# The low parts of the up product's first unit made on GpSimd in place of VectorE, in 54 of 56 expert groups

## The chip, the cores and the metric

The kernel runs on one core of one Trainium2 chip. The metric is the device time of one execution in microseconds (us); below, all times are us unless they say ns. A core has TensorE (PE; its weight loads are shown apart as PEld), VectorE (DVE), ScalarE (ACT), GpSimd (POOL) and SyncE (SP, which here issues the weight transfers). Each engine takes its own instructions in order, and they wait for one another through semaphores. SBUF is the working memory of all of them; PSUM holds what TensorE writes.

## The reference, cut to what matters

Two residual blocks run over 256 tokens of width 1024: first two mLSTM and attention layers, then two layers with a gated mixer each, the first with a dense feed-forward part and the second with a mixture of experts. The change lies in the experts:

```
def moe_swiglu(x, w_router, e_gate, e_up, e_down):
    ...
    top_val, top_idx = lax.top_k(logits, TOP_K)          # 2 of 8 experts for each token
    ...
    for e in range(N_EXPERTS):
        out = out + gates[:, e:e + 1] * swiglu(t, e_gate[e], e_up[e], e_down[e])

def swiglu(x, w_gate, w_up, w_down):
    return (jax.nn.silu(x @ w_gate) * (x @ w_up)) @ w_down
```

The width is 1024, an expert's hidden width 3584, and everything is float32.

## The kernel before

TensorE multiplies parts of float32 numbers. A weight tile `raw` (128 by 2048, 1 MB, called a unit here) is split in two: ScalarE writes its high part, `hi = Copy(raw)` in a shorter format (`high`, L1381), and VectorE writes the remainder, `lo = raw - hi` (`low`, L1385). A product of an expert with many tokens then takes three matmuls for each 128 rows (`mm3`, L242 to L244: hi by x high, lo by x high, hi by x low). For an expert with at most 64 tokens both parts of x lie side by side in one operand, and two matmuls do (L1355 and L1356); two more with a folding matrix (L1406) add up the halves. Which of the two forms runs is a branch on a number computed on the chip.

The expert stage works in 56 **groups**: 8 experts by 7 slices of 512 hidden columns. The list `turns` pairs the experts and alternates between the two of a pair, so that a group of a crowded expert stands beside one of a small expert. A group needs six units: two of the gate matrix (k = 0, u = 0 and 1), two of the up matrix (k = 1) and two of the down matrix (k = 2). They are made in this order; `some(n)` makes the last of group n + 1, the down units of group n and the first three of group n + 2:

```
    high(n + 1, 1, 1); low(n + 1, 1, 1); up(n + 1, 0)
    high(n, 2, 0); turn_hidden(n); high(n, 2, 1); low(n, 2, 0)
    up(n + 1, 1); low(n, 2, 1)
    high(n + 2, 0, 0); low(n + 2, 0, 0); high(n + 2, 0, 1); down(0)
    low(n + 2, 0, 1); high(n + 2, 1, 0); down(1)
    low(n + 2, 1, 0); activate(n + 1)
```

(This is the order without the other steps; the whole function is below.) The stage is recorded under `manual_schedule` for VectorE, ScalarE and TensorE, so these three engines keep the written order. Beside the six `lo`, VectorE does two things in a group, and both read one operand in PSUM: `activate` multiplies the gate by the up product (L1412, `tmp<-tmp,mm`), and `turn_hidden` makes the low part of the transposed hidden tile (L299, `yl<-mm,yh`). A `lo` reads two operands in SBUF. Where a new pair of experts begins there is more: its tokens are picked and gathered (L1285, L1291, L1305 to L1307), and the results of the pair before are added in (`combine`, L1430 and L1431).

The buffers are four `hi`, four `lo` and seven `raw` (four and three in two pools, picked in turn by `raw_tile`). A raw buffer is free when its `lo` is made, and then SyncE issues the next transfer into it (L204). A `hi` or `lo` buffer is free when TensorE has used it. GpSimd has nothing to compute in the expert stage.

Of the kernel before, what the change touches and what calls it, by code (L numbers as in the profile page):

```python
# [10 lines left out]
F32 = mybir.dt.float32  # L11
# [4 lines left out]
OP = mybir.AluOpType  # L16
# [1199 lines left out]
def moe(E, G, p, l, i, out):  # L1216
    nc, tc, I = E.nc, E.tc, E.I
# [150 lines left out]
    raws, w = {}, {}  # L1368
# [13 lines left out]

    def low(n, k, u):
        hi, lo = (x.rearrange("p k n -> p (k n)") for x in w[n, k, u])
        return nc.vector.tensor_tensor(lo, raws.pop((n, k, u)), hi.bitcast(F32), op=OP.subtract)  # L1385

    FIRST = 2
    state = {}
# [53 lines left out]
    for e in range(NEXP):  # L1442
        todo = lambda n, f, *a, of=ahead: of.setdefault(n, []).append((f, a))
        if e:

            n = at[e - 2, nf - 1] - 1 if e > 1 else 0
# [6 lines left out]
        if e % 2 and e + 1 < NEXP:  # L1453
            n = at[e, nf - 1] + 1
# [3 lines left out]
    def some(n):  # L1458
# [19 lines left out]
        if nxt:  # L1478
            high(n + 1, 1, 1)
            low(n + 1, 1, 1)  # L1480
            up(n + 1, 0)
# [3 lines left out]
        turn_hidden(n)  # L1485
        high(n, 2, 1)
        low(n, 2, 0)
        beside_hidden(n)
        if nxt:
            up(n + 1, 1)  # L1490
        low(n, 2, 1)
        if nxt2:
            high(n + 2, 0, 0)
# [202 lines left out]
```

## Time and profile before

| | |
|---|---|
| Time, median of 3 runs | 2000.57 us (2000.23 to 2000.99) |
| Profiled execution: time | 2002.43 us |
| Profiled execution: span, first to last instruction | 2000.1 us |
| TensorE, VectorE, ScalarE, GpSimd busy | 1927.3, 1550.2, 1374.1, 75.7 us |
| The 56 groups, from the first L1412 to the last | 1103.3 to 1971.4 us |
| Expert weights read | 336 units of 1 MB |

A busy time is the union of an engine's instructions. Over the whole span it mixes stages with different limits, so the expert stage is read in stretches of its own. There GpSimd is idle, and TensorE, VectorE, ScalarE and the DMA engines are all busy for most of the time; which of them is waited for changes between stretches. The name in brackets behind a timeline row says what an engine's idle time before that row ended with.

### The profile page before, as it was taken

The page shows a single profiled execution, that of the slowest core. Times are in us where ns is not written, and L with a number is a line of the kernel's source. Part 1 is how long each engine was busy: PE and PEld are TensorE (multiplying, and loading weights), DVE is VectorE, ACT ScalarE, POOL GpSimd, SP SyncE. Part 2 cuts the span into 40 slices and gives each one's busy share as a digit, 9 for nine tenths or more (in the row PEclk, how much of TensorE's full clock was granted, in tenths as well). Part 3 has the DMA queues.
Part 4 walks back from the last instruction along what each step waited for, and adds up shares of the span by engine and source line. Part 5 has one row for each costly group of instructions (what it writes and reads, how often), then busy time and mean ns, then how long its engine had stood idle before and what let it go on. Part 6 is the DMA issues. An engine that isn't in the chain of part 4 may idle for free. (4 is left out here: it accounts for less than half of the span.)

```text
span 2000.1 us, 28105 instructions
## 1 busy us (share of the span) xinstructions
PE 1927.3 (96%) x10164; PEld 1602.2 (80%) x10164; DVE 1550.2 (78%) x1992; ACT 1374.1 (69%) x1932; POOL 75.7 (4%) x109
## 2 busy tenths in 40 slices
PE   8999999999999999999998999999999999999886
PEld 7778998977999887999887787777878787776664
DVE  7857555976555676555867899889999899999996
ACT  7656455756544564444555789888898888989994
POOL 0100000010000210000010000000000000000000
PEclk9999999999999999999998999999999999999998
DMA  7515544534555563555443899999999999999993
GB/s 271 203 43 189 190 169 150 198 132 137 185 187 176 192 220 113 203 211 189 178 171 128 344 398 419 415 357 389 418 418 381 361 418 419 404 358 407 419 420 158
DMA packets 77208, 536.95 MB, mean 268 GB/s; under 512 B 9102, under 2 KB 9376, under 8 KB 13296
## 3 DMA queue, kind: packets, MB, share of 16 engines
q1 hardware_dynamic: 75312, 528.52, 68.7%
q0 software_dynamic: 1296, 6.02, 0.9%
q8 instruction: 111, 1.82, 0.4%
q14 instruction: 57, 0.47, 0.1%
q10 hardware_dynamic: 432, 0.12, 0.0%
HBM read 533.58 MB, written 1.05 MB: 267 GB/s over the span
## 5 line engine op out<-in xcount | busy, mean ns | idle before, releaser
L1385 DVE TENSOR_TENSOR lo<-raw,hi 128x2048 fp32r<-128x2048 f32 x333 | 745.2, 2283 | 33.4 <-ACT hi L1381 33.4
L1381 ACT ACTIVATE hi<-raw 128x2048 fp32r<-128x2048 f32 x333 | 633.6, 1919 | 30.2 <-PE mm L244 12.2
L1041 DVE TENSOR_TENSOR lo<-raw,hi 128x512 fp32r<-128x512 f32 (+2 forms) x696 | 428.2, 666 | 159.4 <-ACT hi L1040 158.9
L1040 ACT ACTIVATE hi<-raw 128x512 fp32r<-128x512 f32 (+2 forms) x696 | 372.5, 602 | 200.0 <-issue 88.8
L243 PE MATMUL acc<-lo,yh 128*128 128x512 f32 x656 | 257.6, 393 | 4.1 <-DVE lo L1385 3.9
L242 PE MATMUL acc<-hi,yh 128*128 128x512 f32 x656 | 258.1, 393 | 0.0
L244 PE MATMUL acc<-hi,yl 128*128 128x512 f32 x656 | 256.5, 391 | 0.0
L190 PE MATMUL mm<-xh,hi 128*128 128x256 f32 x736 | 208.5, 283 | 0.0
L191 PE MATMUL mm<-xl,hi 128*128 128x256 f32 x736 | 208.3, 283 | 0.0
L192 PE MATMUL mm<-xh,lo 128*128 128x256 f32 x736 | 208.3, 283 | 0.0
L242 PE MATMUL mm<-hi,xh 128*128 128x512 f32 x432 | 172.3, 399 | 2.1 <-PEq L1510 1.7
L1355 PE MATMUL mm<-hi,yl 128*128 128x512 f32 x416 | 166.2, 400 | 5.1 <-PEq L1510 4.3
L243 PE MATMUL mm<-lo,xh 128*128 128x512 f32 x432 | 169.3, 392 | 1.6 <-issue 1.6
L244 PE MATMUL mm<-hi,xl 128*128 128x512 f32 x432 | 169.2, 392 | 0.0
L1356 PE MATMUL mm<-lo,yl 128*128 128x512 f32 x416 | 163.1, 392 | 0.0
L243 PEld LDWEIGHTS acc<-lo,yh 128*128 128x128 f32 x656 | 123.4, 188 | 32.9 <-DVE lo L1385 9.0
L244 PEld LDWEIGHTS acc<-hi,yl 128*128 128x128 f32 x656 | 123.2, 188 | 25.2
L242 PEld LDWEIGHTS acc<-hi,yh 128*128 128x128 f32 x656 | 123.5, 188 | 24.7
L191 PEld LDWEIGHTS mm<-xl,hi 128*128 128x128 f32 x736 | 141.2, 192 | 0.6
L190 PEld LDWEIGHTS mm<-xh,hi 128*128 128x128 f32 x736 | 141.2, 192 | 0.6
L192 PEld LDWEIGHTS mm<-xh,lo 128*128 128x128 f32 x736 | 141.2, 192 | 0.0
L242 PE MATMUL acc<-hi,xh 128*128 128x512 f32 x288 | 116.7, 405 | 1.0 <-ACT xh L298 0.6
(339 smaller groups left out, 3055.8 us busy)
## 6 DMA issues: line engine op xcount, KB each, us to landing
raw<-in_exp_w_up_dram SPq DMA_DIRECT2D x112, 1024.0 KB, 8.6
raw<-in_exp_w_gate_dram SPq DMA_DIRECT2D x112, 1024.0 KB, 8.2
raw<-in_exp_w_down_dram SPq DMA_DIRECT2D x112, 1024.0 KB, 8.0
raw<-in_w_in_dram SPq DMA_DIRECT2D x48, 1024.0 KB, 5.0
raw<-in_w_up_dram SPq DMA_DIRECT2D x32, 1024.0 KB, 4.9
raw<-in_w_down_dram SPq DMA_DIRECT2D x32, 1024.0 KB, 4.8
raw<-in_w_out_dram SPq DMA_DIRECT2D x16, 1024.0 KB, 4.9
raw<-in_ffn_w_gate_dram SPq DMA_DIRECT2D x10, 1024.0 KB, 5.6
```

The costliest lines, as they stand in the source:

```text
L190: nc.tensor.matmul(out, lhsT=wh, rhs=ah, start=start, stop=False)
L191: nc.tensor.matmul(out, lhsT=wh, rhs=al, start=False, stop=False)
L192: nc.tensor.matmul(out, lhsT=wl, rhs=ah, start=False, stop=stop)
L242: nc.tensor.matmul(out, lhsT=ah, rhs=wh, start=start, stop=False)
L243: nc.tensor.matmul(out, lhsT=ah, rhs=wl, start=False, stop=False)
L244: nc.tensor.matmul(out, lhsT=al, rhs=wh, start=False, stop=stop)
L1040: a = E.nc.scalar.activation(hi, v, AF.Copy)
L1041: return a, E.nc.vector.tensor_tensor(lo, v, hi.bitcast(F32), op=OP.subtract)
L1355: nc.tensor.matmul(out, lhsT=a[2][:, k, :], rhs=wh, start=f, stop=False)
L1356: nc.tensor.matmul(out, lhsT=a[2][:, k, :], rhs=wl, start=False, stop=l)
L1381: nc.scalar.activation(w[n, k, u][0].rearrange("p k n -> p (k n)"), raws[n, k, u], AF.Copy)
L1385: return nc.vector.tensor_tensor(lo, raws.pop((n, k, u)), hi.bitcast(F32), op=OP.subtract)
```

## The change

`low` chooses its engine. For the first unit of the up matrix, (k, u) = (1, 0), in groups 2 to 55 the subtraction is issued on GpSimd; in groups 0 and 1, and for all other units, it stays on VectorE. Operands and result are the same.

```
     def low(n, k, u):
         hi, lo = (x.rearrange("p k n -> p (k n)") for x in w[n, k, u])
-        return nc.vector.tensor_tensor(lo, raws.pop((n, k, u)), hi.bitcast(F32), op=OP.subtract)
+
+        on = nc.gpsimd if (k, u) == (1, 0) and n >= FIRST else nc.vector
+        return on.tensor_tensor(lo, raws.pop((n, k, u)), hi.bitcast(F32), op=OP.subtract)
```

The file is two lines longer from there on: L1385 becomes L1387, L1412 becomes L1414, and so on. In the following rows, in a steady part of the stage, `lo1601` is the low part that moves, `lo1599` the second gate unit of the same group and `lo1604` the last unit of the group before; `tmp1602` is the product that `activate` makes. VectorE before:

```order
L1385 TENSOR_TENSOR lo1599_14726<-raw1598_14723,hi1599_14725 128x2048
L1361 UNCONDITIONAL_BRANCH
L1385 TENSOR_TENSOR lo1601_14753<-raw1600_14750,hi1601_14752 128x2048
L1412 TENSOR_TENSOR tmp1602_14780<-tmp1602_14780,mm1594_14671 128x512
L1385 TENSOR_TENSOR lo1604_14786<-raw1603_14783,hi1604_14785 128x2048
```

VectorE with the change, at the same place:

```order
L1387 TENSOR_TENSOR lo1599_14726<-raw1598_14723,hi1599_14725 128x2048
L1361 UNCONDITIONAL_BRANCH
L1414 TENSOR_TENSOR tmp1602_14780<-tmp1602_14780,mm1594_14671 128x512
L1361 UNCONDITIONAL_BRANCH
L1387 TENSOR_TENSOR lo1604_14786<-raw1603_14783,hi1604_14785 128x2048
```

VectorE now goes from the second gate unit to the product, and then to the next group's unit; nothing else on it changes its place among the computing instructions. GpSimd with the change, with the semaphores that each row waits for; before, only the branches stood here:

```order
L1361 UNCONDITIONAL_BRANCH x2
L1387 TENSOR_TENSOR lo1601_14753<-raw1600_14750,hi1601_14752 128x2048 [waits DMAHW4_49,Activation_49,Pool_49]
L1361 UNCONDITIONAL_BRANCH x4
L1512 UNCONDITIONAL_BRANCH
L1361 UNCONDITIONAL_BRANCH x2
L1387 TENSOR_TENSOR lo1619_14935<-raw1618_14932,hi1619_14934 128x2048 [waits DMAHW2_49,Activation_49,Pool_49]
```

The moved subtraction has GpSimd to itself, and it starts when ScalarE has made its `hi`. TensorE's order is unchanged; its first matmul with `lo1601` and SyncE's transfer into the freed raw buffer now wait for GpSimd where they waited for VectorE.

## Rows read from the trace of the kernel before

**Rows 1.** Busy engines by stretch of the expert stage, PE clock, DMA share
```profile
core 0: us, PE busy (x) PEld busy (x) DVE busy (x) ACT busy (x) POOL busy (x), PEclk, DMA share, GB/s
1144.00:1265.10 121.10, 118.98 (x536) 96.19 (x535) 115.87 (x65) 108.87 (x92) 0.00 (x0) 1.00 1.00 409
...
1487.70:1590.50 102.80, 101.36 (x476) 81.28 (x475) 91.65 (x60) 89.91 (x85) 0.00 (x0) 1.00 0.96 373
1590.50:1710.40 119.90, 117.67 (x529) 94.97 (x528) 115.71 (x66) 107.49 (x91) 0.00 (x0) 1.00 1.01 418
1710.40:1797.10 86.70, 85.66 (x404) 68.57 (x403) 76.96 (x51) 76.05 (x72) 0.00 (x0) 1.00 0.97 376
1797.10:1883.90 86.80, 79.78 (x341) 58.73 (x339) 86.54 (x50) 80.48 (x70) 0.00 (x0) 1.00 1.00 411
1883.90:1959.70 75.80, 66.44 (x270) 47.33 (x270) 72.67 (x42) 68.53 (x57) 0.58 (x1) 1.00 1.01 420
```

**Rows 2.** Timeline of VectorE over two groups: start, length, instruction, idle before
```profile
1634.85 0.68 DVE L1412 TENSOR_TENSOR tmp<-tmp,mm 128x512 f32<-128x512 f32 x1
...
1638.76 0.69 DVE L299 TENSOR_TENSOR yl<-mm,yh 128x512 fp32r<-128x512 f32 x1 [1.03 <-ACT yh L298]
1639.37 11.13 DVE L1385 TENSOR_TENSOR lo<-raw,hi 128x2048 fp32r<-128x2048 f32 x5
1650.42 0.68 DVE L1412 TENSOR_TENSOR tmp<-tmp,mm 128x512 f32<-128x512 f32 x1
...
1653.82 11.09 DVE L1385 TENSOR_TENSOR lo<-raw,hi 128x2048 fp32r<-128x2048 f32 x5
1664.83 0.68 DVE L1412 TENSOR_TENSOR tmp<-tmp,mm 128x512 f32<-128x512 f32 x1
```

**Rows 3.** Who waited for the lo of L1385, 1144 to 1960: us, times
```profile
  PE acc L243: 3.9, 9
  PE acc L1356: 3.1, 9
  PE mm L1356: 0.8, 1
```

**Rows 4.** What VectorE waited for, 1487.7 to 1590.5: us, times, longest
```profile
DVE lo L1385 <- ACT hi L1381: 7.6, 4, 3.1
DVE yl L299 <- ACT yh L298: 2.2, 4, 1.0
DVE X L1431 <- PE mm L1430: 1.3, 2, 1.0
```

**Rows 5.** Timeline of GpSimd in earlier stages, multiplications with two operands in SBUF
```profile
70.81 0.73 POOL L486 TENSOR_TENSOR tmp<-tmp,rope 128x256 f32<-128x256 f32 x1 [2.96 <-ACT tmp L480]
80.37 2.27 POOL L486 TENSOR_TENSOR tmp<-tmp,rope 128x256 f32<-128x256 f32 x1 [7.94 <-ACT tmp L480]
685.43 1.30 POOL L864 TENSOR_TENSOR ws<-ws,tri 128x512 f32<-128x512 f32 x1 [0.27 <-DMA ws<-in_wsT_dram]
716.27 1.46 POOL L910 TENSOR_TENSOR gg<-gg,srow 128x512 f32<-128x512 f32 x1
720.21 1.30 POOL L864 TENSOR_TENSOR ws<-ws,tri 128x512 f32<-128x512 f32 x1 [2.49 <-DMA ws<-in_wsT_dram]
```

**Rows 6.** Timeline of VectorE at those times
```profile
80.77 0.68 DVE L485 TENSOR_TENSOR tmp<-tmp,rope 128x512 f32<-128x512 f32 x1
81.37 0.68 DVE L1041 TENSOR_TENSOR lo<-raw,hi 128x512 fp32r<-128x512 f32 x1
685.30 1.29 DVE L299 TENSOR_TENSOR xl<-mm,xh 128x512 fp32r<-128x512 f32 x2 [0.34 <-ACT xh L298]
715.88 3.64 DVE L1041 TENSOR_TENSOR lo<-raw,hi 128x512 fp32r<-128x512 f32 x4
```

**Rows 7.** Timeline of ScalarE: the hi of (0,1) and (1,0), then the activation
```profile
1644.07 3.71 ACT L1381 ACTIVATE hi<-raw 128x2048 fp32r<-128x2048 f32 x2
1647.67 0.59 ACT L1411 ACTIVATE tmp<-mm 128x512 f32<-128x512 f32 x1
```

## The prediction, made before the changed kernel was run

> **What bounds the kernel now.** I read the busy times by stretch first, because the whole-span shares mix stages. The change touches only the 56 expert groups, so I cut these at the starts of their L1412 rows. In the steady stretches [rows 1] (1590.5 to 1710.4, eight groups; the one from 1367.9 to 1487.7 is like it, and 1144.0 to 1265.1 nearly) TensorE is busy 98% of the time, VectorE 97%, and the DMA engines move 418 GB/s at a share of 1.01. All three look like the limit. The stretches in which a new pair of experts starts (1487.7 to 1590.5, six groups; 1265.1 to 1367.9 is the same; 1710.4 to 1797.1, five groups) have TensorE at 99% and VectorE at 89%. In the last eleven groups (1797.1 to 1959.7) TensorE falls to 92 and 88% while VectorE has 99.7 and 96%.
>
> VectorE's timeline [rows 2] shows how close it is. The five `lo` in a row take 11.09 us: one is 2.28 us long, and start to start it is (11.09 - 2.28) / 4 = 2.20 us. L1412 and L299 take 0.6 us each, start to start (1638.76 to 1639.37). Six `lo` and these two make 6 x 2.2 + 1.2 = 14.4 us, and the group from 1650.42 to 1664.83 is 14.41 us long: VectorE had no pause at all. The group before took 15.57 us, with one pause of 1.03 us. So VectorE is a bound in these groups, and anything that adds to its line adds to the time; TensorE and DMA follow within a few per cent.
>
> **The change, part by part.** Removed: 54 `lo` on VectorE, 2.2 us each in its line, 119 us in all. Added: 54 subtractions of 128x2048 on GpSimd, which is idle there. No row of before has that operation at that size. The nearest are multiplications with two SBUF operands [rows 5]: 128x256 in 0.73 us and 128x512 in 1.30 us, so (1.30 - 0.73) / 256 = 2.23 ns a column and 0.16 us at the start. For 2048 columns that is 4.7 us; I take 4.6 us of it as the work itself (below). On its own this would be harmless: the result is used a group later.
>
> The question is what VectorE does meanwhile, and the earlier stages show it. At 715.88 VectorE ran four `lo` of 128x512 [rows 6]. Four that are undisturbed would take 3 x 0.6 + 0.68 = 2.48 us; they took 3.64, which is 1.16 us more. GpSimd's multiplication of 128x512 [rows 5] began at 716.27, while the first of them ran. It lasted 1.46 us, 0.16 us more than alone, and ended at 717.73. So GpSimd first waited for the `lo` in progress, and then VectorE stood for GpSimd's whole working time: 1.16 us for 512 columns, 2.27 ns a column. Neither ran beside the other. For 2048 columns that makes 4.6 us. At 685.30 it was otherwise: two VectorE subtractions whose first operand is in PSUM (L299) took 1.29 us for two, so 0.6 us each as elsewhere, right beside GpSimd's L864 [rows 5, 6]. So I take it that a `lo`, with both operands in SBUF, and the new GpSimd subtraction exclude one another, and that L299 and L1412 do not mind.
>
> Where in the group does the 4.6 us fall? GpSimd can start when its `hi` is made. In the group of [rows 2] ScalarE made the `hi` of (0,1) and (1,0) from 1644.07 on and was done at 1647.78 [rows 7]. VectorE's five `lo` began at 1639.37, so the fourth, of (0,1), ran from 1645.97 to 1648.2 and the fifth, the moved one, from 1648.2. GpSimd is thus ready while the fourth runs and gets its turn at 1648.2, just where VectorE's own would have started. VectorE can then run L1412 (0.6 us, PSUM) and stands before the next `lo`. Its line per group is five `lo` (11.0), L1412 and L299 (1.2) and 4.6 for GpSimd, less the 0.6 of L1412 beneath it: **16.2 us in place of 14.4, +1.8 us**. The pauses of about 1 us for `yh` in every other steady group go away, since VectorE then comes later than TensorE. The waits that move to GpSimd (TensorE's first matmul with this `lo`, SyncE's next transfer, a later `hi` of ScalarE) come most of a group after GpSimd is done, and are costed at nothing; a group that is over 1 us longer also leaves the transfers more room.
>
> The sum by stretches: the three steady ones have 24 groups, 24 x 16.2 = 388.8 us against 121.1 + 119.8 + 119.9 = 360.8: **+28**. The last eleven groups last 162.6 us. 11 x 16.2 = 178.2 is +16; but both experts of this pair are small, TensorE is done with its buffers sooner, and GpSimd may be ready before the fourth `lo` begins. Then nothing is hidden and a group is 16.8 us, +22. I take **+19**. In the 17 groups of the three other stretches VectorE waits already, 11.1 us in six groups [rows 4]; GpSimd can work within such a wait. Of the six, one has no wait (+1.8) and one only 0.5 us (+1.3): at least 3 us a stretch, at most 6 x 1.8 = 10.8. I take 5, 5 and 4, together **+14**. The first two groups, which fill the pipeline, get nothing. Together 28 + 19 + 14 = +61 us. The profiled execution took 2002.4 us (span 2000.1), so 2063 us; the median of the runs is 1.9 us lower, and the forecast for it is **2062 us**.
>
> **Two rules of the Trainium skill against these rows.** Its page "GPSIMD Engine Reference" (section 3, Performance versus the Vector engine) gives 4497 ns for a float32 addition of this size on GpSimd, which would be 0.1 us less a group than my 4.6, some 4 us less in the sum. Its page "SBUF — State Buffer" (SBUF: two separate sides) says that VectorE with two SBUF inputs and GpSimd share a pair of ports as a lock, which whoever starts first holds for its whole instruction. The trace agrees on the standing still (1.16 us for 512 columns), but not on the turn: at 80.37 GpSimd's 128x256 took 2.27 us in place of 0.73, while two VectorE instructions that started after it, at 80.77 and 81.37, ran at their usual 0.68 [rows 5, 6]. By first come, the last pair costs 22 and the total is 64; if VectorE may go ahead as at 80.37, GpSimd gets in at L1412 in every group, the last pair costs 16, and the total is 58.
>
> **Rivals.** *They do not exclude one another in this form* (the other side). VectorE's line would fall to 12.2 us a group. For it: the GpSimd rows are multiplications with float32 results, not subtractions to the shorter format. Against it: the 1.16 us above. The time would then go to the next limits. Six units are 6.29 MB; at the 418 to 420 GB/s of [rows 1] that is 15.0 us, and the steady groups take (15.57 + 14.41) / 2 = 14.99. So nothing is gained there: 1998 to 2001 us, no measurable change. It decides from the point where GpSimd's turn costs VectorE under 2.2 us.
>
> *Nothing is hidden*: L1412 stands too, or GpSimd's turn falls between two `lo` everywhere, and the waits in the gather stretches absorb nothing. Then a group is 16.8: 28 + 24 x 0.6 = 42, 17 x 1.8 = 31, and 22, so +95: 2096 us. *More is hidden*, L299 as well as L1412, 15.6 us a group: 24 x 15.6 = 374.4 (+14), 171.6 (+9), and some 4 in the gather stretches: +27, 2028 us.
>
> *Faster*: without exclusion and with DMA able to do more than these rows show, TensorE's own waits for `lo` could go, 7.8 us in all [rows 3]: 1993 us. Both conditions are needed, and 1.01 of DMA share speaks against the second.
>
> **How the numbers follow.** Exclusion with a group of 15.6 to 16.8 us: 0.86, most likely near 16.2, so 2062, with the bounds of the hidden part 2028 and 2096. No exclusion: 0.10 without a gain, 0.04 with one. The range leaves out the rivals without exclusion and the outer part of "nothing hidden": 2024 to 2092. A measurement of this kernel can tell about 0.2% (4 us) from no change. Faster 0.04, same 0.09, slower 0.87.
>
> **What would show it.** Right: GpSimd rows of about 4.6 to 5 us, or longer where they wait for their turn; one `lo` a group that takes 6 us or more in place of 2.28, the first behind L1414; steady groups of about 16.2 us without waits for `yh`; DMA at 6.29 MB / 16.2 us = 388 GB/s; TensorE waiting for `lo` more than before. Wrong: `lo` at 2.28 us beside a busy GpSimd; the long one behind L299 or in the middle of the five; groups in the gather stretches that grow as much as the steady ones. TensorE's clock shows 1.00, its 2.4 GHz level, in the last groups with TensorE at 88% [rows 1], about as idle as a group of 16.2 us would leave it (118 / 130 = 91%), so I expect no fall to 1.2 GHz; longer single waits would break that and make it slower still.

## The result, and the profile after

The changed kernel takes **2066.73 us** (median of 5 runs, 2063.84 to 2069.66), against 2000.57 us before (5 runs, 2000.23 to 2002.02): a ratio of 1.0333, with a 95% interval of 1.0322 to 1.0344. The forecast was 2062 us with a range of 2024 to 2092. The profiled execution of after is the fastest of its five (2063.84 us, span 2062.0), and its span is 61.9 us longer than the one of before.

L1387 is now the line of every `lo`, L1413 and L1414 are the activation's two lines (L1411 and L1412 before). Cut 0.04 us ahead of the starts of the L1414 rows, which end the same groups as the cuts of [rows 1], the stretches are these (columns as in [rows 1]):

```profile
core 0: us, PE busy (x) PEld busy (x) DVE busy (x) ACT busy (x) POOL busy (x), PEclk, DMA share, GB/s
1145.75:1272.68 126.93, 120.28 (x531) 95.24 (x530) 119.17 (x56) 108.52 (x92) 44.27 (x9) 1.00 0.97 378
...
1509.40:1617.91 108.51, 103.01 (x475) 80.70 (x474) 94.27 (x53) 89.85 (x85) 32.13 (x7) 1.00 0.92 350
1617.91:1746.11 128.20, 120.67 (x531) 95.12 (x530) 120.53 (x57) 108.56 (x92) 45.63 (x9) 1.00 0.99 392
1746.11:1840.63 94.52, 88.70 (x407) 69.03 (x406) 81.86 (x46) 78.47 (x73) 31.78 (x6) 1.00 0.93 353
1840.63:2018.03 177.40, 150.77 (x606) 113.11 (x606) 172.73 (x78) 145.92 (x127) 57.84 (x10) 0.94 0.98 381
```

The rows of eight groups went from 121.1 and 119.9 us to 126.9 and 128.2, those in which a pair of experts starts from 102.8 and 86.7 to 108.5 and 94.5, and the last eleven groups from 162.6 to 177.4. VectorE now makes one `lo` a group fewer, yet its busy time in eight groups rose (115.7 to 120.5 us). GpSimd, idle there before, is busy 5.7 us a group. TensorE fell from 98 to 94%, DMA from 418 to 392 GB/s. So neither of these two became the bound; VectorE's line got longer. Its timeline shows where:

```profile
1641.15 8.88 DVE L1387 TENSOR_TENSOR lo<-raw,hi 128x2048 fp32r<-128x2048 f32 x4
1649.96 0.68 DVE L1414 TENSOR_TENSOR tmp<-tmp,mm 128x512 f32<-128x512 f32 x1
1651.40 5.25 DVE L1387 TENSOR_TENSOR lo<-raw,hi 128x2048 fp32r<-128x2048 f32 x1 [0.77 <-ACT hi L1381]
1656.57 0.68 DVE L299 TENSOR_TENSOR yl<-mm,yh 128x512 fp32r<-128x512 f32 x1
1657.17 8.88 DVE L1387 TENSOR_TENSOR lo<-raw,hi 128x2048 fp32r<-128x2048 f32 x4
1665.98 0.67 DVE L1414 TENSOR_TENSOR tmp<-tmp,mm 128x512 f32<-128x512 f32 x1
```

GpSimd's timeline over the same group:

```profile
1649.21 5.29 POOL L1387 TENSOR_TENSOR lo<-raw,hi 128x2048 fp32r<-128x2048 f32 x1 [10.73 <-ACT hi L1381]
1664.45 6.09 POOL L1387 TENSOR_TENSOR lo<-raw,hi 128x2048 fp32r<-128x2048 f32 x1 [9.96 <-ACT hi L1381]
```

Read the two together. GpSimd asks at 1649.21 (its row of 5.29 us, against 4.56 for the shortest of them, holds a wait for its turn), while the last of VectorE's four `lo` runs. That `lo` ends at 1650.03 (1641.15 + 8.88), GpSimd's row at 1654.50: 4.47 us. In them VectorE does L1414 and then stands. Its next `lo` begins at 1651.40, ends at 1656.65, and has its usual 2.2 us only from about 1654.4 on. The four behind it are undisturbed (8.88 us for four). The group takes 16.02 us in place of 14.4 to 15.6.

The result has a reader sooner than forecast. TensorE's timeline of that group, its first matmul with the moved unit:

```profile
1654.55 0.50 PE L1356 MATMUL mm<-lo,yl 128*128 128x512 f32 x1 [1.18 <-POOL lo L1387]
```

TensorE had come to it 1.18 us before GpSimd was done. Its waits for the moved unit from 1150 to 2020 (us in total, times, longest):

```profile
PE mm L1356 <- POOL lo L1387: 37.2, 28, 1.9
```

What VectorE waits for in the six groups that start a pair (1509.4 to 1617.9; before: [rows 4]):

```profile
DVE tmp L1414 <- ACT tmp L1413: 5.9, 2, 3.0
DVE lo L1387 <- ACT hi L1381: 5.4, 7, 1.7
DVE X L1433 <- PE mm L1432: 1.6, 2, 1.0
DVE yl L299 <- ACT yh L298: 1.2, 1, 1.2
```

That is 14.1 us in all, where it was 11.1.

| stretch | before | after | difference | forecast |
|---|---|---|---|---|
| first two groups | 40.73 | 42.55 | +1.8 | 0 |
| three steady stretches, 24 groups | 360.84 | 383.32 | +22.5 | +28 |
| three gather stretches, 17 groups | 292.25 | 311.56 | +19.3 | +14 |
| last eleven groups | 162.58 | 177.40 | +14.8 | +19 |
| the last interval, group 54 to 55 | 11.68 | 15.53 | +3.9 | 0 |

The cut between the last two of the long stretches hides something: the first of the last eleven groups takes 12.60 us in place of 14.41. It is the sixth after a pair starts, and in the two other gather stretches the sixth took 13.99 in place of 15.9. Counted with its stretch, the gather groups cost 17.5 and the last ten groups 16.6.

### The profile page after: what moved, and what is told of

It is laid out like the page before. It is cut to its first block, busy times and chain, and to the rows that moved or that the text cites. A ratio compares the mean times of both kernels' runs of the same rounds, so it can differ in the third digit from the quotient of the medians.

```text
span 2062.0 us, 28109 instructions
## 1 busy us (share of the span) xinstructions
PE 1947.9 (94%) x10164; PEld 1609.1 (78%) x10164; DVE 1591.5 (77%) x1938; ACT 1375.4 (67%) x1932; POOL 374.9 (18%) x163
## 5 line engine op out<-in xcount | busy, mean ns | idle before, releaser
L1387 DVE TENSOR_TENSOR lo<-raw,hi 128x2048 fp32r<-128x2048 f32 x279 | 782.4, 2844 | 47.3 <-ACT hi L1381 47.3
L1387 POOL TENSOR_TENSOR lo<-raw,hi 128x2048 fp32r<-128x2048 f32 x54 | 300.0, 5556 | 610.4 <-ACT hi L1381 610.3
L1356 PE MATMUL mm<-lo,yl 128*128 128x512 f32 x416 | 171.9, 413 | 37.5 <-POOL lo L1387 27.8
L243 PEld LDWEIGHTS acc<-lo,yh 128*128 128x128 f32 x656 | 123.7, 189 | 37.8 <-DVE lo L1387 13.9
```

Source lines behind the costliest of these rows:

```text
L243: nc.tensor.matmul(out, lhsT=ah, rhs=wl, start=False, stop=False)
L1356: nc.tensor.matmul(out, lhsT=a[2][:, k, :], rhs=wl, start=False, stop=l)
L1387: return on.tensor_tensor(lo, raws.pop((n, k, u)), hi.bitcast(F32), op=OP.subtract)
```

## The experiments

The theory under test: GpSimd's two-operand subtraction and VectorE's `lo` exclude one another, so a moved column saves VectorE 1.04 ns (a `lo` of 128x512 takes 0.6 us of its line, one of 128x2048 2.2, so (2.2 - 0.6) / 1536) and costs it about 2.2 ns. The main rival: they don't, and the time comes from the result being late for TensorE, or from writes.

**GpSimd writes as long, but reads almost nothing** (e1_write_only). One column of the moved `lo` is subtracted, the others are filled; `behind` keeps each instruction after the one before. (In the edits below, `...` stands for lines left out.)

```diff
...
+        i = nc.gpsimd.tensor_tensor(lo[:, 0:1], raw[:, 0:1], hi[:, 0:1].bitcast(F32), op=OP.subtract)
+        for end in (2048, 2048, 768):
+            with behind(E, [i]):
+                i = nc.gpsimd.memset(lo[:, 1:end].bitcast(F32), 0.0)
```

> The moved subtraction is replaced on GpSimd by one column of it and three constant fills of the same tile (2047, 2047 and 767 columns), so the tile is ready about as late as with the change, but GpSimd reads almost nothing from SBUF; the product then works with fills in place of the low parts. Theory (VectorE stands while GpSimd reads two SBUF operands): VectorE's line falls to 12.2 us a group and its lo stay at 2.28 us; the next limit is DMA, 1996 to 2004 us. Rival (the tile comes late and TensorE waits for it): as with the change, 2062 to 2068 us. If a GpSimd write alone also stops VectorE: 2062 too, but with lo of over 5 us.

Measured: 2013.79 us, ratio 1.0067 (1.0051 to 1.0084). GpSimd's row and VectorE's rows beside it:

```profile
1444.89 4.50 POOL L1392 MEMSET lo<- 128x2047 f32 x3
```
```profile
1445.38 0.69 DVE L1419 TENSOR_TENSOR tmp<-tmp,mm 128x512 f32<-128x512 f32 x1 [0.47 <-ACT tmp L1418]
1447.18 2.29 DVE L1388 TENSOR_TENSOR lo<-raw,hi 128x2048 fp32r<-128x2048 f32 x1 [1.12 <-ACT hi L1381]
```

The `lo` at 1447.18 lies beside GpSimd's last two fills and takes its usual 2.29 us; of all 279 none took over 2.295. So a GpSimd that writes as long and is about as late costs 13 us, not 66. The theory had counted on 1996 to 2004 and missed the lateness: TensorE waits 32.8 us for GpSimd's tile in 31 places, and the three steady stretches are 3.9 us longer than before, the three gather stretches 5.9, the last interval 3.5.

**One fill** (e4_short_write): as above with a single fill, so GpSimd is done 2.7 us sooner.

```diff
-        for end in (2048, 2048, 768):
-            with behind(E, [i]):
-                i = nc.gpsimd.memset(lo[:, 1:end].bitcast(F32), 0.0)
+        with behind(E, [i]):
+            nc.gpsimd.memset(lo[:, 1:2048].bitcast(F32), 0.0)
```

> One fill of 2047 columns in place of the moved subtraction: VectorE is relieved of one lo a group, and the tile is ready about 2 us after its hi, sooner than before the change. It bounds what relieving VectorE of this lo could bring. If DMA at 419 GB/s is the next limit: 1995 to 2001 us. If VectorE alone was the limit: 24 groups down from 15.0 to 14.7 (TensorE's 29.4 a pair) and the last eleven from 14.8 to 12.8 or so: 1970 us.

Measured: 1995.51 us, 0.9978 (0.9969 to 0.9988), the steady stretches 4.0 us shorter than before. That is about all that freeing VectorE of one `lo` a group brings here: its line falls to 12.2 us a group, but the steady groups still take 14.9 on average. TensorE is 99% busy in them and DMA moves 419 to 420 GB/s, so there either can be the bound; in the last groups, of 14.9 us too, TensorE is at 88% and DMA at 419 GB/s. The run with three fills took 18 us more than this one: that is what 2.7 us of lateness cost without the exclusion.

**GpSimd copies in place of subtracting** (e2_one_input): the three fills of the first run become copies from `raw`, one operand to read.

```diff
-                i = nc.gpsimd.memset(lo[:, 1:end].bitcast(F32), 0.0)
+                i = nc.gpsimd.tensor_copy(lo[:, 1:end], raw[:, 1:end])
```

> As the run with fills, but three copies of the weight tile in their place (2047, 2047 and 767 columns): GpSimd reads one SBUF operand. The product works with copies in place of low parts. If any GpSimd read of SBUF stops VectorE's subtractions: lo of 4 us and more, and 2050 to 2085 us, depending on how long a copy takes (an estimate from 0.79 us for 512 columns: 2.5 to 3 us for 2047). If only two operands do: about 2000 us. The rival (lateness) expects 2062 us or more, with lo at 2.28 us.

Measured: 2178.38 us, 1.0894 (1.0876 to 1.0913), above the range given for an exclusion. The rival of lateness had named 2062 or more, with `lo` at 2.28 us; 202 of the 279 `lo` took about that, the others up to 3.89. Three copies took 6.7 to 8.8 us; TensorE waited 129 us for the copies in 30 places, and ScalarE paused 148 us ahead of its `hi` for nothing that the profile shows. The run has several causes at once (late results, and a raw buffer held for the length of three copies), and these it doesn't separate. So the question was put again with one copy.

**One copy** (e9_short_copy): the single fill of 2047 columns becomes a single copy.

```diff
-            nc.gpsimd.memset(lo[:, 1:2048].bitcast(F32), 0.0)
+            nc.gpsimd.tensor_copy(lo[:, 1:2048], raw[:, 1:2048])
```

> GpSimd makes one column of the moved lo as a subtraction and copies the other 2047 columns from the raw unit (the subtraction of those columns is left out), so it has one SBUF operand to read in place of two, and the same columns to write as the single fill of the run before with 1995.5 us. Theory A, one-operand reads of GpSimd do not meet VectorE's two-operand lo: no lo over 2.4 us, copies near 1.9 us, total 1994 to 1998. Theory B, they exclude each other as the subtractions do: a lo of 4 us or more in most groups, or copies of 4 us, and steady groups of 12.2 + 1.9 - 0.6 = 13.5 to 14.1 us by VectorE's line, which is still no more than DMA's 14.9: total 1995 to 2001. The durations of the rows decide, not the total.

Measured: 1995.84 us, 0.9977 (0.9968 to 0.9986), the same as with the fill. The rows decide. In 47 of 54 groups the copy lies beside the activation's product and VectorE's wait for `hi`, and meets no `lo` for more than 0.3 us. In the other seven a `lo` came while the copy ran. One of them, GpSimd's row and VectorE's:

```profile
1817.44 1.90 POOL L1391 CAST lo<-raw 128x2047 fp32r<-128x2047 f32 x1
```
```profile
1817.37 0.68 DVE L1418 TENSOR_TENSOR tmp<-tmp,mm 128x512 f32<-128x512 f32 x1
1818.20 3.28 DVE L1388 TENSOR_TENSOR lo<-raw,hi 128x2048 fp32r<-128x2048 f32 x1 [0.16 <-ACT hi L1381]
```

The same place of the run with one fill:

```profile
1818.08 1.81 POOL L1391 MEMSET lo<- 128x2047 f32 x1
```
```profile
1818.89 2.29 DVE L1388 TENSOR_TENSOR lo<-raw,hi 128x2048 fp32r<-128x2048 f32 x1 [0.19 <-ACT hi L1381]
```

Beside the copy the `lo` takes 1.00 us more, of the 1.14 us for which the copy still ran; beside the fill nothing. All seven agree (2.67 to 3.28 us there, 2.29 with the fill). The L1418 product, with one operand in PSUM, takes 0.68 beside either. So reading one operand excludes a `lo` too, and only writing does not: theory B in the rows, without an effect on the total.

**The exclusion with nobody waiting for the result** (e3_extra): VectorE makes all six `lo`, and GpSimd subtracts pieces of `hi` into a tile that nobody reads.

```diff
...
+            for c in range(0, 2048, 512):
+                x, y = (hi[:, o:o + 512].bitcast(F32) for o in (c, (c + 512) % 2048))
+                nc.gpsimd.tensor_tensor(extra, x, y, op=OP.subtract)
...
```

> VectorE makes all six lo as before; GpSimd, in groups 2 to 55, makes four extra subtractions of 512 columns (two slices of the same hi) into a tile that nobody reads. Theory: VectorE's line is 14.4 + 4.5 - 0.6 = 18.3 us in a steady group: 24 x 18.3 - 361 = +78, 11 x 18.3 - 163 = +39, and some 50 in the 17 others: 2165 us, 2130 to 2190. Rival (lateness): nobody waits for the extra tile, 2000 us.

Measured: 2160.99 us, 1.0803 (1.0785 to 1.0821), 4 us from the theory's number and 160 from the rival's. That close it is by luck: the steady stretches cost 67 us (78 expected), the last eleven groups 31 (39), the gather stretches 56 (some 50) and the first two groups 6 (none). The rows:

```profile
1430.27 11.45 POOL L1389 TENSOR_TENSOR extra<-hi 128x512 f32<-128x512 f32 x4 [6.18 <-ACT hi L1381]
```
```profile
1420.15 13.80 DVE L1390 TENSOR_TENSOR lo<-raw,hi 128x2048 fp32r<-128x2048 f32 x5
1433.88 0.67 DVE L1419 TENSOR_TENSOR tmp<-tmp,mm 128x512 f32<-128x512 f32 x1
1434.47 2.79 DVE L1390 TENSOR_TENSOR lo<-raw,hi 128x2048 fp32r<-128x2048 f32 x1
```

Four pieces take 11.45 us because GpSimd gets its turns between VectorE's `lo`; the five `lo` take 13.80 in place of the 11.09 of [rows 2], and L1419 still 0.67. VectorE doesn't pause in this group: its longer rows alone make it 17.6 us in place of 14.4, and that is the exclusion by itself. Elsewhere the run isn't so pure. Nobody reads `extra`, but ScalarE waits for the `hi` buffer that GpSimd still reads:

```profile
ACT hi L1381 <- POOL extra L1389: 191.6, 50, 6.7
```

In most steady groups VectorE never stands for that; in the gather stretches it does wait for `hi`, and there the run doesn't tell the two apart.

**Smaller pieces** (e6_split_256, e6_split_512): GpSimd makes only the first 256 or 512 columns of the unit, VectorE the rest.

```diff
...
+            nc.gpsimd.tensor_tensor(lo[:, 0:256], raw[:, 0:256], hi[:, 0:256].bitcast(F32), op=OP.subtract)
+            lo, raw, hi = lo[:, 256:2048], raw[:, 256:2048], hi[:, 256:2048]
```

> GpSimd makes 256 of the 2048 columns, VectorE the other 1792. GpSimd's turn is 0.56 us, which L1414 (0.6 us) covers; VectorE saves 256 / 0.96 GHz = 0.27 us a group, 14.1 us. Theory: 1995 to 2000 us, at best what the short fill gave (1995.5). If each turn costs more than its columns: 2001 us or more.

> 512 columns on GpSimd, 1536 on VectorE. GpSimd's turn is 1.12 us, 0.5 us of it beyond L1414; VectorE saves 0.53 us. Theory: even, 14.4 us a group, 1997 to 2004 us; above the run with 256 columns by 0 to 6 us.

Measured: 2004.35 us, 1.0019 (1.0010 to 1.0028), and 2009.10 us, 1.0044 (1.0031 to 1.0058); both above what was expected. The steady groups that VectorE bounds take 14.7 and 15.0 us in place of 14.41: 256 columns save 256 x 1.04 ns = 0.27 us and cost 256 x 2.2 = 0.56, 512 save 0.53 and cost 1.12. The expectation had again hidden a part beneath the activation. But here VectorE's own part of the same unit stands ahead of the activation, so GpSimd's turn falls between two `lo`, where nothing is hidden. In the first five of the last eleven groups it was otherwise: with 256 columns GpSimd asked in the fourth `lo`, let the fifth pass and got its turn at L1417.

```profile
1853.59 4.30 POOL L1388 TENSOR_TENSOR lo<-raw,hi 128x256 fp32r<-128x256 f32 x1 [9.84 <-ACT hi L1381]
1857.22 0.68 DVE L1417 TENSOR_TENSOR tmp<-tmp,mm 128x512 f32<-128x512 f32 x1
```

These five took 14.14 us, the 0.27 less that the expectation counted on. Over the whole run neither size gains.

**The change again** (e5_again), for the spread of its runs.

> The change itself once more, for a second profile. In the first one two of the last groups took 20.4 us with 14.0 us after, where GpSimd got its turn between two lo, in place of 16.0 and 16.0: 2.4 us more each time. If such turns make the spread of the runs (2063.8 to 2069.7), a run's time is about 2059 + 2.4 us for each long group in its profile, and the times lie between 2059 and 2071 us.

Measured: 2068.94 us, 1.0339 (1.0323 to 1.0354). In the last eleven groups the first profile of the change has two groups of 20.4 us and this one four; each is followed by one of 13.9 to 14.4. That pair takes 34.4 to 34.8 us, 2.4 to 2.8 more than two of 16.0, and the stretch is 183.13 us long in place of 177.40. By what was expected, four such pairs make 2068.6 us; the profiled run took 2070.37. The first such pair of the first profile, VectorE then GpSimd:

```profile
1940.46 13.28 DVE L1387 TENSOR_TENSOR lo<-raw,hi 128x2048 fp32r<-128x2048 f32 x4
1953.67 0.68 DVE L1414 TENSOR_TENSOR tmp<-tmp,mm 128x512 f32<-128x512 f32 x1
1954.26 2.28 DVE L1387 TENSOR_TENSOR lo<-raw,hi 128x2048 fp32r<-128x2048 f32 x1
1958.31 0.69 DVE L299 TENSOR_TENSOR yl<-mm,yh 128x512 fp32r<-128x512 f32 x1 [1.77 <-ACT yh L298]
```
```profile
1947.02 4.58 POOL L1387 TENSOR_TENSOR lo<-raw,hi 128x2048 fp32r<-128x2048 f32 x1 [9.23 <-ACT hi L1381]
```

GpSimd asked one `lo` early, at 1947.02, in the third of the four, and got its turn before the last (13.28 us, where four take 8.88). The 4.4 us that VectorE stands reach TensorE. Its windows about that place (columns as in [rows 1]):

```profile
1949.50:1953.50 4.00, 0.00 (x0) 0.00 (x0) 4.00 (x1) 1.84 (x2) 2.10 (x1) 1.00 0.99 420
1954.00:1957.00 3.00, 3.00 (x8) 2.23 (x9) 2.54 (x2) 0.00 (x0) 0.00 (x0) 0.50 0.78 238
1953.67:1967.72 14.05, 13.83 (x54) 10.63 (x54) 12.28 (x8) 10.53 (x10) 1.31 (x1) 0.88 0.94 339
1840.67:1853.27 12.60, 12.47 (x59) 10.29 (x60) 12.29 (x8) 11.53 (x13) 0.97 (x1) 1.00 0.93 368
```

TensorE had no matmul for 4 us, and the clock granted next is 0.50, its 1.2 GHz level, for about 3 us. The group behind is then bound by TensorE (13.83 of 14.05 us); a group as short at clock 1.00, the last row, took 12.60. By this comparison about 1.4 of the 2.4 us of this pair are the clock's, and the rest is the part that is not hidden.

**A later `hi`, so that GpSimd never asks early** (e7_later_hi): on ScalarE the moved unit's `hi` is made behind the activation.

```diff
-            high(n + 2, 1, 0)
         down(1)
...
-        if nxt2:
-            low(n + 2, 1, 0)
         if nxt:
             activate(n + 1)
+        if nxt2:
+            high(n + 2, 1, 0)
+            low(n + 2, 1, 0)
```

> The change, but ScalarE makes the moved unit's hi after the activation instead of before it, 0.6 us later, so that GpSimd asks for its turn when VectorE is already in the lo of (0,1), the last before L1414. Theory: no group of 20.4 us, no pause for yh behind it, 2057 to 2063 us and little spread. If the turns are not decided by when GpSimd asks: 2062 to 2070 with the same spread.

Measured: 2126.60 us, 1.0632 (1.0616 to 1.0649): far off. The long groups are gone (the last ones take 16.5 us each), but the steady groups grew to 17.4. Two rows of its waits:

```profile
DVE lo L1387 <- ACT hi L1381: 116.9, 57, 3.5
ACT tmp L1413 <- PE mm L1408: 98.0, 32, 8.4
```

The activation waits for TensorE, and the `hi` now stands behind it on ScalarE. GpSimd asks only when L1414 is half done (at 1472.31, L1414 from 1471.92), and holds VectorE for nearly all of 4.6 us with nothing to hide beneath: a group of 16.4 us. In the groups of 17.9 us beside these it asks later still, 1.2 us after L1414 (at 1455.83), and VectorE stands for that as well.

**The last transfer out of GpSimd's queue** (e8_rows_by_SyncE). In the changed kernel the last `lo` stands on GpSimd behind a transfer of `rows` (L1048) that waits 11.9 us for its buffer:

```profile
2018.45 0.58 POOL L1048 DMA_DIRECT2D rows<-in_srow_dram  x1 [11.85 <-DMA raw<-in_exp_w_down_dram]
2019.05 4.56 POOL L1387 TENSOR_TENSOR lo<-raw,hi 128x2048 fp32r<-128x2048 f32 x1
```

```diff
-    E.nc.gpsimd.dma_start(row, E.I["srow"][l, c:c + 2048].partition_broadcast(P))
+    (on or E.nc.gpsimd).dma_start(row, E.I["srow"][l, c:c + 2048].partition_broadcast(P))
...
-    g, b_ = norm_rows(E, p, l, 3584, "rawx", 3)
+    g, b_ = norm_rows(E, p, l, 3584, "rawx", 3, nc.sync)
```

> The change whole, and the last norm's rows (the transfer of L1048 into a rawx buffer) are asked for by SyncE in place of GpSimd. Theory: after the change GpSimd's queue puts the last lo behind that transfer, which waits for its buffer, and this alone costs the last interval (product of L1414 of group 54 to that of 55) 3.85 us. Moved to SyncE's queue, where no lo stands behind it, the interval falls from 15.5 to 12 to 13 us, and the rest of the run is as with the change: 2060 to 2067 us. Rival: the last interval is longer because the last lo comes late for another reason (VectorE's turn); then it stays at 15 us or more.

Measured: 2067.59 us, 1.0333 (1.0319 to 1.0348), and a last interval of 14.51 us in place of 15.53: 1.0 us of the 3.9, where 2.5 to 3.5 were expected. VectorE's timeline of that interval has the remaining cause:

```profile
2023.95 0.67 DVE L1414 TENSOR_TENSOR tmp<-tmp,mm 128x512 f32<-128x512 f32 x1
2025.04 5.58 DVE L1387 TENSOR_TENSOR lo<-raw,hi 128x2048 fp32r<-128x2048 f32 x1 [0.42 <-ACT hi L1381]
```

Without the transfer ahead of it GpSimd still takes its turn at L1414, and the next `lo` stands for 3.3 us (5.58 - 2.28). Most of the 2.8 us that stay is this, by the size of the two; it was not tried apart. This profile has four long groups as well (last stretch 182.97 us), so the total can't show one us.

## Why the prediction held, point by point

**VectorE as the bound, and the exclusion** are shown: by the stretched `lo` behind L1414, by the groups of e3_extra in which VectorE never pauses, and by the split runs, whose steady groups follow saved columns x 1.04 ns against moved columns x 2.2 ns. The Trainium skill's page "SBUF — State Buffer" (SBUF: two separate sides) tells the lock as one of VectorE with two SBUF inputs against a GpSimd operation that reads SBUF; the fill that stops nothing and the copy that does are both as it says.

**The hold, 4.6 us**, is 4.47 in the row of 1649.21; alone GpSimd takes 4.56 us at the least in that profile. The stretched `lo` itself is 4.9 to 5.3 us in the steady groups, where 6 or more was named as the sign; the 0.7 to 1.1 us before it, put down to `hi`, lie beneath the turn as well and make 6.0. The steady group of 16.2 us came out at 16.0 (15.9 in the first of the three stretches), and these 24 groups at +22.5 in place of +28. For the hold, the figure that the Trainium skill's page "GPSIMD Engine Reference" (section 3) gives for an addition of this size, 4497 ns, was nearer than 4.6 us.

**Where the hold falls**, at the activation with L1414 beneath, is right in the steady groups: the `yh` waits are gone there (from 1618 to 1746 VectorE waits for `hi` alone, 7.7 us), and DMA runs at 378 and 392 GB/s where 388 were forecast.

**"GpSimd can work within such a wait"** is the step that failed, the one behind the +14 of the gather stretches. VectorE's waits there are still 14.1 us in six groups. Half of the 11.1 us of before, 2.52 and 3.06 us, stood right ahead of the moved `lo` itself, whose `hi` ScalarE had not made yet (the `lo` just before L1412):

```profile
1519.90 2.29 DVE L1385 TENSOR_TENSOR lo<-raw,hi 128x2048 fp32r<-128x2048 f32 x1 [2.52 <-ACT hi L1381]
1553.44 2.29 DVE L1385 TENSOR_TENSOR lo<-raw,hi 128x2048 fp32r<-128x2048 f32 x1 [3.06 <-ACT hi L1381]
```

GpSimd needs that same `hi`, so it can't work within such a wait. With the change, at the end of the second of the six groups:

```profile
1543.59 1.90 ACT L1381 ACTIVATE hi<-raw 128x2048 fp32r<-128x2048 f32 x1
1545.62 4.62 POOL L1387 TENSOR_TENSOR lo<-raw,hi 128x2048 fp32r<-128x2048 f32 x1 [14.69 <-ACT hi L1381]
1546.00 0.69 DVE L1414 TENSOR_TENSOR tmp<-tmp,mm 128x512 f32<-128x512 f32 x1 [3.00 <-ACT tmp L1413]
1548.38 4.01 DVE L1387 TENSOR_TENSOR lo<-raw,hi 128x2048 fp32r<-128x2048 f32 x1 [1.69 <-ACT hi L1381]
```

The `hi` is done at 1545.49, and 0.4 us after GpSimd's start the wait of 3.00 us is over; the turn, until 1550.24, lies behind it. Beneath it are L1414 and the next wait for `hi`, and the `lo` after that still stands for 1.7 us. So the groups grew by 1.6, 0.6, 0.6, 1.5 and 3.4 us (15.31 to 16.91, 19.08 to 19.64, 15.99 to 16.61, 17.55 to 19.02, 18.90 to 22.33), and the sixth alone gives 1.9 back: together 5.8 us in six groups against 7.5 in eight steady ones, as much a group, which the prediction had named as a sign against it. The term was to be 14 and is 19.3, or 17.5 with its sixth group.

**"Most of a group after GpSimd is done"** was wrong as well: TensorE stands for the moved unit in 28 places. In the steady groups that is 4.0 us in eight and isn't on the path, since VectorE there has no pause outside GpSimd's turn. The last interval was left out for the same reason and is +3.9: 1.0 of it is the queue, most of the rest the hold. How much the lateness has of the gather groups wasn't separated; without the exclusion (e1_write_only) these stretches were 5.9 us longer than before and 7.2 longer than with one fill. The first two groups, which were to get nothing, hold GpSimd's first turn, again behind a wait for the moved unit's own `hi` (3.46 us before): the first took 1.7 us less, the second 3.5 more.

**The last eleven groups** were to cost 16 to 22 us, "GpSimd may be ready before the fourth `lo` begins". That happens in two groups of the first profile and in four of the change run again: +14.8 and +20.6. The spread of the runs goes with it: the first profile stands at the lower end of the runs (2063.84) and the median 3 us above it.

**The clock.** "No fall to 1.2 GHz" is right for the steady and gather stretches (1.00 throughout) and wrong for the last pair of experts: 0.94 over the stretch, with a piece of 0.50 in the windows above. In most of those groups VectorE is the bound and the lower clock costs nothing (groups of 16.0 us at 0.89 and at 1.00 alike); in the short group behind a long one it costs about 1.4 us.

So the sum was right to 1 us in the profiled executions (61.9 us between the spans, +61 forecast) because terms too high (steady, 5.5, and the last groups of the profiled run, 4.2) and too low (gather, 5.3, the ends, 5.7) nearly cancel, which is luck; the median of the runs lies another 3 us higher. The sign was right for the reason given, and so was the main term, 28 us forecast and 22.5 measured.

## What to carry to other kernels

Before work goes from a full VectorE to an idle GpSimd, count what each of them reads from SBUF: in these runs a VectorE instruction with two operands in SBUF stood for as long as GpSimd read SBUF, so a moved column cost VectorE 2.2 ns and saved it 1.04. Beside VectorE instructions with an operand in PSUM (0.68 us either way), or as a mere write, GpSimd's work cost VectorE nothing, and even then the next bounds (here DMA and TensorE) left only 0.2% to gain. A result that moves to a slower engine also comes later: follow it to its first reader, and look at what else stands in that engine's queue, before its wait is costed at nothing. And a wait is no room for the moved work when it is a wait for that work's own operand.

## What the runs showed of the hardware beyond that

GpSimd's turn isn't by one simple order in these traces: at 80.37 [rows 5, 6] it stood while two later VectorE instructions ran, at 1853.59 of the run with 256 columns it let another `lo` pass; at 1947.02 it came in between two `lo`, as its pieces did in e3_extra. What decides this was not settled.
